# Routing by replaced maxima, filler products in TensorE's waits, a first gather in four PSUM banks, and the norm's factors moved

## The chip, the cores and the metric

The kernel runs on one core of a Trainium2 chip, in one launch. Its time is the device time of that core in microseconds (us). One core's TensorE (PE), VectorE (DVE), ScalarE (ACT) and GpSimd (POOL) work beside each other, each in the order of its own program; SyncE (SP) issues nearly all of the DMAs, in order, and DMAs are also issued from POOL.

## The reference

Two transformer blocks run one after the other over 256 tokens of width 1024, in fp32. The last part of the second block is a mixture of 32 experts, and the change lies where that part begins:

```python
h = layer_norm(DEEPNORM_ALPHA * h + m, ln1_g[l], ln1_b[l])
f = moe_ffn(h, ...)
h = layer_norm(DEEPNORM_ALPHA * h + f, ln2_g[l], ln2_b[l])

# moe_ffn
logits = (t @ w_router + b_router).astype(jnp.float32)     # 32 experts
top_val, top_idx = lax.top_k(logits, TOP_K)                # 4 of them for a token
gate_w = jax.nn.softmax(top_val, axis=-1)
hb = xb @ w_exp_in[e] + b_exp_in[e]                        # xb: the tokens of expert e
g = jnp.minimum(hb[:, :D_FF_2], SWIGLU_LIMIT)
u = jnp.clip(hb[:, D_FF_2:], -SWIGLU_LIMIT, SWIGLU_LIMIT)
a = g * jax.nn.sigmoid(SWIGLU_ALPHA * g) * (u + 1.0)
return a @ w_exp_out[e] + b_exp_out[e]
y = jnp.einsum('nk,nkd->nd', gate_w, y_slot)
```

Every expert has 12 MB of weights, and all 32 are read from HBM.

## The kernel before

**Weights.** `Stream` (`ws`) holds all weights as a list of 2 MB tiles: 42 of the dense stages, then six for each of the 32 experts (four for the hidden layer, two for the output). A tile goes to SBUF when one of the buffers in the list `ws.free` is named for it; SP issues the loads in that order, in `ahead` (L69). Each load waits until the buffer's former reader is done. Ten buffers hold expert tiles: three `ring` buffers `w0` to `w2`, three `wh0` to `wh2` that held split halves in the dense stages, `ring2` (`w`, which holds the gates `gt` until L832 has read them), `ring3` (`w`), and two in the pool `more4` (L1030), which is opened where the buffers of the earlier stages were closed. The first two experts are fixed, so their weights need no routing; for the others SP reads the expert's number from `ids` (L152).

**The stage before the experts** (t is a block of 128 tokens, 0 or 1). `rows_n` (L264) ends the product with `w_out` in four PSUM banks `acc`. L894 adds ALPHA times the block's input into `xn` on DVE and sums it. PE turns `xn` to feature-major (L900), ACT or DVE copies that to `zt` (L902, L904), ACT squares for the variance (L907), POOL takes the power -0.5 (L189), and PE multiplies `zt` with the router's weights (L912). The norm's factors are already in `wrg`; what they add to the logits is in `cr`, from eight products of L843. On DVE, L914 and L865 make the normed rows `hn` with both factors, whose rows `ln` POOL loads as 128 copies (L840).

**Routing.** `chosen(t)` ends the logits (L868, L869), takes the eight largest (L870), their places (L871), compares the places of the first four with 0 to 31 (L872) and adds them up to `sel` (L874). L923 and L925 count the tokens of each expert ahead of each token, L927 makes positions of that, and `one_hots` (L882) makes the selection matrix of experts 0 and 1. `gather(0)` (L1051) picks their tokens with 16 products, each out of 128 features and two token blocks. Then the four gate weights (L936 to L945, in buffers of the pool `rp`), `sort_experts` (L964 to L991, experts in order of their count), and the gates' rows (L1058) come before the first expert.

**The experts.** For each expert `hidden` multiplies the picked tokens with the weights (L1073), `gated` applies the activation (L1090 to L1100), `out_rows` (L1109) and `scatter` (L1124) end it. Experts have 32, 64 or 128 slots (`SLOTS`); experts of less than 128 slots use two or four parts of the array at once. `SORT` lists the places inside the experts' loop where a further step of `sort_experts` is put. Within each engine the order is set by a scheduler, apart from blocks under `manual_schedule` and waits put in by `after`.

## Time and profile before

| | |
|---|---|
| median of 3 runs | 1451.88 us (1450.11 to 1451.99) |
| profiled execution, its own time | 1451.97 us |
| its span from the first to the last instruction | 1450.2 us |
| TensorE busy | 1378.8 us (95%) |
| VectorE busy | 661.0 us (46%) |
| ScalarE busy | 429.4 us (30%) |
| GpSimd busy | 35.6 us (2%) |
| HBM read | 492.68 MB |
| mean over the span | 340 GB/s |

TensorE's busy time counts matmuls that are pipelined and whose ends are modelled, so a high share does not show that TensorE is the limit. The dense stages take about the first 500 us of the span, the experts nearly all of the rest.

### The profile page before, as it was taken

Reading aid. Unit: us, or ns where it says so; the run is one execution under the profiler, and the core shown is the slowest. Engines: PE = TensorE matmul, PEld = TensorE weight load, DVE = VectorE, ACT = ScalarE, POOL = GpSimd, SP = SyncE. Lnnn points to the kernel's source line nnn. Section 1 sums busy time; section 2 is a strip of 40 time slices with the busy share of each in tenths; the row PEclk is TensorE's granted clock in tenths of the full one; section 3 lists DMA queues with packets and bytes.
Section 4 is the critical chain, followed back from the end, with each engine's and each line's share of the span. In section 5 each row is a group of like instructions: output and inputs, shape, how many; then the busy total and the mean of one; then the engine's idle time right before and its main releaser. Section 6 shows DMA issues by size and latency. Waiting matters only on the chain. (4 is left out here: it accounts for less than half of the span.)

```text
span 1450.2 us, 21020 instructions
## 1 busy us (share of the span) xinstructions
PE 1378.8 (95%) x8401; PEld 869.7 (60%) x8402; DVE 661.0 (46%) x1614; ACT 429.4 (30%) x805; POOL 35.6 (2%) x53
## 2 busy tenths in 40 slices
PE   8999999999999989999999999999999999998884
PEld 7988999979999844444444444453544444443432
DVE  5868877865776543233233223233223333232223
ACT  4535655544664212121112112112111121211112
POOL 1001000010001000000000000000000000000000
PEclk9999999999999999999999999999999999999998
DMA  8434554445535989999999999999999999999995
GB/s 353 155 146 176 220 195 175 180 178 191 204 125 183 394 357 402 425 427 426 427 428 426 426 427 428 427 426 427 426 428 427 426 428 426 425 428 427 425 427 213
DMA packets 38007, 495.15 MB, mean 341 GB/s; under 512 B 4560, under 2 KB 4880, under 8 KB 8592
## 3 DMA queue, kind: packets, MB, share of 16 engines
q1 hardware_dynamic: 35424, 486.69, 81.1%
q0 software_dynamic: 2192, 6.88, 1.4%
q8 instruction: 68, 1.11, 0.3%
q14 instruction: 35, 0.29, 0.1%
q10 hardware_dynamic: 288, 0.18, 0.0%
HBM read 492.68 MB, written 1.05 MB: 340 GB/s over the span
## 5 line engine op out<-in xcount | busy, mean ns | idle before, releaser
L1073 PE MATMUL m<-w,xs 128*64 128x512 f32 (+2 forms) x1456 | 316.0, 601 | 12.6 <-DMA w<-in_wexp_dram 12.6
L1090 DVE TENSOR_TENSOR gu<-m,bexp 128x256 f32<-128x256 f32 (+2 forms) x128 | 51.2, 400 | 431.6 <-PE m L1087 282.9
L1073 PEld LDWEIGHTS m<-w,xs 128*64 128x64 f32 (+2 forms) x1456 | 101.9, 134 | 179.6 <-issue 169.9
L1076 ACT COPY hs<-m 128x512 f32<-128x512 f32 x128 | 75.1, 586 | 440.4 <-PE m L1073 440.4
L232 PE MATMUL b<-ah,wh 128*128 128x256 f32 x1552 | 195.4, 283 | 1.8 <-ACT wh L83 1.4
L232 PEld LDWEIGHTS b<-ah,wh 128*128 128x128 f32 x1552 | 188.3, 191 | 5.6 <-ACT wh L83 1.8
L105 DVE TENSOR_TENSOR wh<-w,wh 128x1024 fp32r<-128x1024 f32 (+1 forms) x152 | 174.3, 1180 | 28.2 <-ACT wh L104 28.2
L104 ACT ACTIVATE wh<-w 128x1024 fp32r<-128x1024 f32 (+1 forms) x154 | 148.9, 1020 | 87.9 <-PE b L232 53.4
L1109 PE MATMUL m<-w,ea 128*32 128x512 f32 (+2 forms) x704 | 154.0, 619 | 7.1 <-DMA w<-in_wexp_dram 4.4
L1073 PE MATMUL m<-wh,xs 128*32 128x512 f32 (+2 forms) x592 | 112.0, 597 | 2.3 <-DMA wh<-in_wexp_dram 2.3
L232 PE MATMUL b<-al,wh 128*128 128x256 f32 x776 | 100.6, 282 | 0.0
L1097 ACT ACTIVATE ea<-gu 128x128 f32<-128x128 f32 (+2 forms) x128 | 38.5, 301 | 209.4 <-DVE gu L1095 209.4
L205 DVE SCALAR_TENSOR_TENSOR one<-m,gs,one 128x512 fp32r<-128x512 f32 x64 | 46.8, 749 | 114.3 <-ACT one L204 112.8
L232 PEld LDWEIGHTS b<-al,wh 128*128 128x128 f32 x776 | 95.7, 192 | 0.0
L1109 PEld LDWEIGHTS m<-w,ea 128*32 128x32 f32 (+2 forms) x704 | 45.4, 133 | 83.5 <-issue 62.9
L1124 PE MATMUL acc<-one,so 128*128 128x512 f32 x256 | 78.3, 425 | 11.3 <-ACT one L204 10.1
L1085 PEld LDWEIGHTS m<-fold,hs 128*128 128x128 f32 x448 | 54.6, 192 | 46.9 <-issue 34.1
L1124 PEld LDWEIGHTS acc<-one,so 128*128 128x128 f32 x256 | 43.0, 188 | 51.6 <-ACT one L204 32.0
L1109 PE MATMUL m<-wh,ea 128*64 128x512 f32 (+2 forms) x320 | 70.4, 611 | 2.7 <-DMA wh<-in_wexp_dram 2.3
L204 ACT ACTIVATE one<-m,gs 128x512 fp32r<-128x512 f32 x64 | 42.5, 686 | 94.3 <-PE m L1109 94.3
L1073 PEld LDWEIGHTS m<-wh,xs 128*32 128x32 f32 (+2 forms) x592 | 33.7, 126 | 59.2 <-issue 57.2
L1051 PE MATMUL m<-oneh,hn 128*128 128x96 f32 (+2 forms) x480 | 64.5, 283 | 0.0
(358 smaller groups left out, 1351.0 us busy)
## 6 DMA issues: line engine op xcount, KB each, us to landing
w<-in_wexp_dram SPq DMA_DIRECT2D x134, 2048.0 KB, 27.2
wh<-in_wexp_dram SPq DMA_DIRECT2D x57, 2048.0 KB, 27.8
w<-in_wpre_dram SPq DMA_DIRECT2D x37, 2048.0 KB, 7.9
w<-in_wpre_dram SPq DMA_DIRECT2D x4, 512.0 KB, 7.8
w<-in_wexp_dram SPq DMA_DIRECT2D x4, 512.0 KB, 30.1
tab<-in_tab_dram SPq DMA_DIRECT2D x1, 1152.0 KB, 10.2
xn<-in_x_dram SPq DMA_DIRECT2D x2, 512.0 KB, 4.8
ra<-in_rowv_dram POOLq DMA_DIRECT2D x2, 512.0 KB, 7.1
```

Source lines behind the costliest of these rows:

```text
L104: self.nc.scalar.activation(h[:, c], t[:, c], AF.Copy)
L105: self.nc.vector.tensor_tensor(l[:, c], t[:, c], h[:, c].bitcast(F32), op=OP.subtract)
L204: return (A.activation(hi, src, AF.Copy, scale=scale), V.scalar_tensor_tensor(lo, src, scale, hi.bitcast(F32), op0=OP.mult, op1=OP.subtract))
L205: V.scalar_tensor_tensor(lo, src, scale, hi.bitcast(F32), op0=OP.mult, op1=OP.subtract))
L232: T.matmul(p[:, m, :], x[:, k, c], y[:, k, :], start=i == m == k == 0, stop=i == 2 and k == nk - 1, skip_group_check=True)
L1051: T.matmul(b[:, kk], hn[:, t, f], oh[:, t].rearrange("p i c -> p (i c)")[:, 128 - c0:128 + c1], start=t == 0, stop=t == 1)
L1073: T.matmul(b[g * c:(g + 1) * c], xs[:, k, :], w[:, kk, :], start=k < n, stop=k >= 8 - n, skip_group_check=True)
L1076: A.copy(h, b)
L1085: T.matmul(p[:, j, :], h[:, j * 128:(j + 1) * 128], fold, start=True, stop=True)
L1090: V.tensor_tensor(both, p[:, :, 0:c], bexp[:, r, f].rearrange("p j i -> p (j i)")[:, :, None].to_broadcast([128, 4, c]), op=OP.add)
L1109: T.matmul(ys[n][g * c:(g + 1) * c], ac[:, kk, :], w[:, kk, n * 512:(n + 1) * 512], start=(j == kk == 0) if c == 128 else j < 64 // c, sto ...
L1124: T.matmul(acc[t][n], so[:, t * 128:(t + 1) * 128], y[:, n, :], start=first and y is yh, stop=last and y is yl, skip_group_check=True)
```

## The change

- **Router.** The norm's two factors go to other places. `wsum` adds up `wrg` over the eight feature groups on DVE, so that `cr` needs one product and not eight. Mean and variance come from `bn_stats`, not from sums and ACT's squares. The eight router products write four parts of one bank, and a product with `fold` adds the four parts.
- **Rows.** `hn` is the normed row without factors, made by ACT. The 128 copies of the factors' rows are not loaded. The first four experts' tokens get the factors per feature when they are copied from PSUM (`factored`); `hn` itself gets them in a later step of `sort_experts`, from two single rows that PE spreads over the partitions.
- **Selection.** `chosen` replaces the four largest logits by a very small number (`match_replace`) and compares with the logits. The softmax works on all 32 logits, with the others multiplied by zero, in the experts' loop.
- **First gather.** Block 0 is counted, placed and picked ahead of block 1, into the four banks that held `acc`; block 1 adds to them.
- **Order.** `awake` multiplies `ones` with `iota` into banks that nobody reads then, at three places. Of `sort_experts` the counts and comparisons come early, `ids` inside the first expert's first hidden product, the rest in the loop. The pool `more4` is opened on the other side of SBUF.

```diff
-SORT = ((0, 1), (0, 2), (2, 1), (2, 3), (18, 1), (20, 1))
+SORT = ((0, 1), (0, 2), (0, 3), (2, 1), (2, 3), (18, 1), (20, 1))
...
-    ln = single.tile([128, 2, D], F32, name="one")
     ws.free.append((ring2, "w"))
-    for i in range(2):
-        nc.gpsimd.dma_start(ln[:, i, :], a["rowv"][4 + i:5 + i, :].to_broadcast([128, D]))
+
+    wsum = rp.tile([128, 2, E], F32, name="wsum")
+    V.tensor_reduce(wsum, wrg.rearrange("p i k e -> p i e k"), axis=AX.X, op=OP.add)
     cs = ps.tile([128, 2, E], F32, name="b")
-    for k in range(8):
-        T.matmul(cs, ones, wrg[:, :, k, :], start=k == 0, stop=k == 7)
+    T.matmul(cs, ones, wsum, start=True, stop=True)
...
         V.max(v8[:, t, :], logits[:, t, :])
-        V.max_index(i8[:, t, :], v8[:, t, :], logits[:, t, :])
-        V.tensor_tensor(oneh[:, t], iota[:, None, 0:E].to_broadcast([128, K4, E]),
-                        i8[:, t, 0:K4, None].to_broadcast([128, K4, E]), op=OP.is_equal)
-        return V.tensor_reduce(sel[:, t, :], oneh[:, t].rearrange("p k e -> p e k"), axis=AX.X, op=OP.add)
...
+        V.memset(v8[:, t, K4:], 3.4e38)
+        V.match_replace(left[:, t, :], v8[:, t, :], logits[:, t, :], -3.4e38)
+        return V.tensor_tensor(sel[:, t, :], logits[:, t, :], left[:, t, :], op=OP.is_gt)
...
+    def pick(t, ks):
+
+        for k in ks:
+            done = T.matmul(picked[k // 2][:, k % 2 * 128:k % 2 * 128 + 128], hn[:, t, k * 128:(k + 1) * 128],
+                            first[:, t].rearrange("p i c -> p (i c)")[:, 128 - caps(0):128 + caps(1)],
+                            start=t == 0 and k % 2 == 0, stop=t == 1, skip_group_check=True)
+        return done
+
+    def awake(b, n=1):
+
+        for _ in range(n):
+            done = T.matmul(b[:, 0:256], ones, iota[:, 0:256], start=True, stop=True, skip_group_check=True)
+        return done
...
+        for n in range(2):
+            V.scalar_tensor_tensor(xn[:, t, half[n]], xn[:, t, half[n]], ALPHA, acc[t][n], op0=OP.mult, op1=OP.add)
+            V.bn_stats(st[:, n, :], xn[:, t, half[n]])
+        V.bn_aggr(mean[:, t, :], st.rearrange("p n s -> p (n s)"))
...
-        with after(*[copied] if t else ()):
-            A.activation(junk, xn[:, t, :], AF.Square, bias=nmu[:, t:t + 1], accum_out=ve)
...
+                grouped = T.matmul(b[g:g + E], wrg[:, 0, k, :], zt[:, k, t * 128:(t + 1) * 128], start=k < 4, stop=k > 3, skip_group_check=True)
...
+            behind = grouped, T.matmul(b, groups, fold, start=True, stop=True)
...
-        V.scalar_tensor_tensor(hn[:, t, :], xn[:, t, :], nmu[:, t:t + 1], ln[:, 0, :], op0=OP.add, op1=OP.mult)
...
+        with after(copied if t else summed):
+            A.activation(hn[:, t, :], xn[:, t, :], AF.Identity, scale=lr[t], bias=minus[:, t:t + 1])
+        if t:
+            places_of(0, ahead[0])
+        chosen(t)
+    picked = acc[0] + acc[1]
+    with after(behind[1]):
+        done = pick(0, range(5))
     with after(done):
...
+        ahead = prefix(1)
+    placed = places_of(1, ahead[0])
+    with after(ahead[1]):
+        done = pick(0, range(5, 8))
     with after(done):
...
+        done = awake(ps.tile([128, 256], F32, name="b"))
+    with after(done):
+        pick(1, range(8))
...
+    more = pool(ctx, "more4", side="right")
...
+            if scalar:
+                A.activation(xs[:, k, :], src(k), AF.Identity, scale=g, bias=b)
+            else:
+                done = V.tensor_scalar(xs[:, k, :], src(k), g, b, op0=OP.mult, op1=OP.add)
...
+        for i, op in enumerate((OP.mult, OP.add)):
...
+                T.matmul(b, ones[32 * i:32 * i + 1, :], bw[32 * i:32 * i + 1, half[n]], start=True, stop=True)
+                for t in range(2):
+                    V.tensor_tensor(hn[:, t, half[n]], hn[:, t, half[n]], b, op=op)
```

The first place is SP's queue where the last of the expert loads of the dense stages and the two into `more4` stand. Before (`wh0` to `wh2` are the former halves, `w0_5361` and `w1_5363` are the two buffers of `more4`; a wait on DMAHW is on an earlier load of that semaphore):

```order
L69 DMA w1_5119<-in_wexp_dram 128x4096 [waits DMAHW6_49,DVE_49]
L69 DMA w_5359<-in_wexp_dram 128x4096 [waits DMASW3_49,DMASW4_49,DMASW2_49,DMASW5_49,DMASW1_49,DMASW6_49,DMASW0_49,DMASW7_49,PE_49,Pool_49]
L69 DMA wh0_5353<-in_wexp_dram 128x4096 [waits PE_49]
L69 DMA wh1_5355<-in_wexp_dram 128x4096 [waits PE_49]
L69 DMA wh2_5357<-in_wexp_dram 128x4096 [waits PE_49]
L69 DMA w0_5361<-in_wexp_dram 128x4096 [waits DMASW4_49,DMASW5_49,DVE_49,DMASW6_49,PE_49,DMAHW7_49,Activation_49,Pool_49]
L69 DMA w1_5363<-in_wexp_dram 128x4096 [waits DMAHW0_49]
L152 TENSOR_LOAD ids_4736 [waits DMASW3_49,DMASW2_49,DMASW4_49,DMASW1_49,DMASW5_49,DMASW0_49,DMASW6_49,DVE_49,DMASW7_49,Activation_49,Pool_49]
```

The same place of the changed kernel, where the load after the two into `more4` is `w2_5373`:

```order
L70 DMA w1_5111<-in_wexp_dram 128x4096 [waits DMAHW6_49,DVE_49]
L70 DMA wh0_5337<-in_wexp_dram 128x4096 [waits PE_49]
L70 DMA wh1_5339<-in_wexp_dram 128x4096 [waits PE_49]
L70 DMA wh2_5341<-in_wexp_dram 128x4096 [waits PE_49]
L70 DMA w0_5345<-in_wexp_dram 128x4096 [waits DMAHW7_49,PE_49,Activation_49]
L70 DMA w1_5347<-in_wexp_dram 128x4096 [waits DMAHW0_49]
L70 DMA w2_5373<-in_wexp_dram 128x4096 [waits DMAHW1_49,PE_49]
L153 TENSOR_LOAD ids_4736 [waits DMASW3_49,DMASW2_49,DMASW4_49,DMASW1_49,DMASW5_49,DMASW0_49,DMASW6_49,DVE_49,DMASW7_49,Activation_49,Pool_49]
```

The first load into `more4` no longer waits for DVE or POOL, only for PE and ACT, and one more load stands ahead of the reading of `ids`, where ten register loads stood ahead of that load before.

The second place is DVE from the end of the selection of block 1 to the last op that `rp` holds. Before (`hn_4720` rows are L865, `ex` and `oneh_5128` lie in `rp`):

```order
L874 TENSOR_REDUCE sel_4732<-oneh_5128 128x32 [waits DVE_49]
L865 SCALAR_TENSOR_TENSOR hn_4720<-hn_4720,l11_5227,one_5027 128x512
L927 SCALAR_TENSOR_TENSOR pg_4729<-b_5251,sel_4732 128x64 [waits DVE_49,PE_49]
L882 TENSOR_SCALAR oneh_5256<-iota_4721,pg_4729 128x128 [waits DVE_49]
L882 TENSOR_SCALAR oneh_5256<-iota_4721,pg_4729 128x128 x3
L865 SCALAR_TENSOR_TENSOR hn_4720<-hn_4720,l11_5227,one_5027 128x512
L932 COPY posm_4731<-pg_4729 128x2x2
L936 TENSOR_TENSOR ex_5263<-v8_5126 128x8
```

In the changed kernel, the same stretch (`left` is the row with its four largest replaced, `b_5266` the count ahead):

```order
L866 MAX v8_5116<-pg_4729 128x8 [waits DVE_49]
L867 MEMSET v8_5116 128x4 [waits DVE_49]
L868 MATCH_REPLACE left_5117<-v8_5116,pg_4729 128x32 [waits DVE_49]
L869 TENSOR_TENSOR sel_4732<-pg_4729,left_5117 128x32 [waits DVE_49]
L902 SCALAR_TENSOR_TENSOR pg_4729<-b_5266,sel_4732 128x32 [waits DVE_49,PE_49]
L878 TENSOR_SCALAR oneh_5118<-iota_4721,pg_4729 128x128 [waits DVE_49]
L878 TENSOR_SCALAR oneh_5118<-iota_4721,pg_4729 128x128
L991 TENSOR_SCALAR ea_5299<-b_5269,sortc_4727 32x32 [waits DMASW1_49,DMASW6_49,PE_49,Activation_49]
L993 SCALAR_TENSOR_TENSOR ea_5299<-b_5269,sortc_4727 32x32
L994 TENSOR_TENSOR ea_5299<-ea_5299 32x128 [waits DVE_49]
L1007 TENSOR_SCALAR xs0_5303<-acc01_5035,colv_68 128x128 [waits PE_49]
```

No op on `hn` and no gate weight stands there any more, and two of the four one-hot ops are gone from behind block 1's count.

The third place is PE from the gather to the first hidden product. Before (`acc00`, `acc01` serve as the gather's banks; the counts L923, L925 and L964 stand ahead):

```order
L1051 MATMUL acc00_5284<-oneh_5256,hn_4720 128x128 [waits DVE_49]
L1051 MATMUL acc01_5285<-oneh_5256,hn_4720 128x128
L1051 MATMUL acc01_5285<-oneh_5256,hn_4720 128x128 [waits DVE_49]
L1051 MATMUL acc01_5285<-oneh_5256,hn_4720 128x128 x6
L1051 MATMUL acc00_5284<-oneh_5256,hn_4720 128x128 [waits DVE_49]
L1051 MATMUL acc00_5284<-oneh_5256,hn_4720 128x128 x6
L978 MATMUL m_5317<-ones_69,ea_5303 128x2 [waits DVE_49,Activation_49]
L986 MATMUL m_5333<-perm_5321,ea_5303 32x32 [waits DVE_49]
L987 MATMUL m_5333<-perm_5321,cn_5299 32x32
L1058 MATMUL m_5340<-gtok_4730,oneh_5256 128x2 x2
L1058 MATMUL m_5346<-gtok_4730,oneh_5256 128x2 x2
L1073 MATMUL m_5352<-w2_4908,xs0_5307 64x512 [waits DMAHW7_49,PE_49,Activation_49]
```

In the changed kernel (block 1's counts, and ahead of them five of block 0's eight picks, stand just ahead; L916 is a filler of `awake`, L1145 the first hidden product):

```order
L908 MATMUL acc10_5036<-oneh_5118,hn_4720 128x128
L908 MATMUL acc11_5037<-oneh_5118,hn_4720 128x128 x2
L916 MATMUL b_5280<-iota_4721,ones_69 128x256
L908 MATMUL acc00_5034<-oneh_5118,hn_4720 128x128 [waits DVE_49,Activation_49]
L908 MATMUL acc00_5034<-oneh_5118,hn_4720 128x128
L908 MATMUL acc01_5035<-oneh_5118,hn_4720 128x128 x2
L908 MATMUL acc10_5036<-oneh_5118,hn_4720 128x128 x2
L908 MATMUL acc11_5037<-oneh_5118,hn_4720 128x128 x2
L1025 MATMUL m_5329<-ones_69,ea_5299 128x2 [waits DVE_49,DMASW5_49,PE_49,Pool_49]
L1145 MATMUL m_5336<-w2_4908,xs0_5303 64x512 [waits DMAHW7_49,Activation_49]
```

Behind block 1's count stand 11 picks and a filler instead of 16 picks, and the sort's two products and the gates' four have moved behind the first hidden products.

## Rows read from the trace of the kernel before

**Rows 1.** The page: what the DMA engines moved, GB/s in 40 slices of the span

```profile
GB/s 353 155 146 176 220 195 175 180 178 191 204 125 183 394 357 402 425 427 426 427 428 426 426 427 428 427 426 427 426 428 427 426 428 426 425 428 427 425 427 213
```

**Rows 2.** Stretches: us, busy us and count by engine, granted clock, DMA share, GB/s

```profile
464.00:478.60 14.60, 14.60 (x121) 14.34 (x120) 14.60 (x36) 7.58 (x12) 0.00 (x0) 1.00 0.76 290
...
483.00:500.00 17.00, 17.00 (x79) 13.87 (x78) 1.67 (x6) 2.32 (x4) 1.62 (x3) 1.00 1.01 424
...
511.00:518.00 7.00, 6.04 (x42) 5.76 (x42) 4.91 (x21) 0.79 (x2) 0.00 (x0) 0.74 0.45 142
518.00:560.00 42.00, 41.23 (x215) 18.87 (x215) 14.42 (x55) 6.45 (x13) 0.00 (x0) 1.00 0.99 408
...
600.00:1000.00 400.00, 393.57 (x2000) 186.96 (x1998) 118.35 (x396) 69.43 (x142) 0.00 (x0) 1.00 1.01 427
1000.00:1400.00 400.00, 378.09 (x2076) 170.35 (x2072) 121.08 (x416) 71.33 (x148) 0.00 (x0) 0.99 1.01 427
```

**Rows 3.** What SP's queue waited for, 460 to 560 us: total, times, longest

```profile
SPq L69 <- DVE pg L944: 13.9, 1, 13.9
...
SPq L69 <- DVE one L832: 6.6, 1, 6.6
...
SPq L152 <- DVE ids L988: 2.5, 1, 2.5
```

**Rows 4.** SP's timeline, single loads: start, duration of the issue

```profile
477.69 0.33 SPq L69 DMA_DIRECT2D w<-in_wexp_dram  x1
...
500.63 0.33 SPq L69 DMA_DIRECT2D wh<-in_wexp_dram  x1
...
515.15 0.33 SPq L69 DMA_DIRECT2D w<-in_wexp_dram  x1
...
524.82 0.33 SPq L69 DMA_DIRECT2D w<-in_wexp_dram  x1
...
551.30 0.33 SPq L69 DMA_DIRECT2D wh<-in_wexp_dram  x1
```

**Rows 5.** DMA issues: count, KB each, median us to landing

```profile
one<-in_rowv_dram POOLq DMA_DIRECT2D x2, 512.0 KB, 13.1
```

**Rows 6.** DVE's groups by shape, 463 to 520 and 1400 to 1451 us: busy, mean ns

```profile
L874 DVE TENSOR_REDUCE sel<-oneh 128x32 f32<-128x128 f32 x2 | 0.7, 368 | 0.1
...
L944 DVE TENSOR_REDUCE pg<-oneh 128x64 f32<-128x256 f32 x1 | 0.6, 590 | 0.0
...
L871 DVE FIND_INDEX8 i<-v,logits 128x8 uint32<-128x32 f32 x2 | 0.4, 179 | 0.0
...
L1183 DVE BATCH_NORM_STATS2 st<-acc 128x6 f32<-128x512 f32 x2 | 1.3, 690 | 0.9 <-PE acc L1124 0.9
```

**Rows 7.** Timeline of the routing, 475 to 527 us: start, duration

```profile
475.43 1.89 PE L843 MATMUL b<-wrg,ones 128*128 128x64 f32 x16
...
502.22 0.68 DVE L894 SCALAR_TENSOR_TENSOR xn<-xn,acc 128x512 f32<-128x512 f32 x1
...
504.61 1.15 ACT L907 ACTIVATE al<-xn,nmu 128x1024 f32<-128x1024 f32 x1 [1.22 <-DVE nmu L896]
...
507.73 0.57 POOL L189 TENSOR_TENSOR l<-ve,mhalf 128x1 f32<-128x1 f32 x1
...
509.47 0.37 DVE L874 TENSOR_REDUCE sel<-oneh 128x32 f32<-128x128 f32 x1
...
511.83 5.16 PE L1051 MATMUL acc<-oneh,hn 128*128 128x128 f32 x32
...
519.38 7.09 PE L1073 MATMUL m<-w,xs 128*64 128x512 f32 x32
```

**Rows 8.** Short stretches of the routing, columns as in rows 2

```profile
506.00:507.00 1.00, 0.41 (x4) 0.30 (x3) 1.00 (x7) 0.00 (x0) 0.00 (x0) 1.00 1.12 475
...
508.00:510.00 2.00, 0.11 (x1) 0.11 (x1) 1.54 (x7) 0.00 (x0) 0.29 (x1) 0.50 1.03 434
...
515.00:517.00 2.00, 2.00 (x19) 1.88 (x18) 0.15 (x1) 0.59 (x1) 0.00 (x0) 1.00 0.56 106
```

More of the change, by code (lines that the diff above doesn't have):

```diff
@@ L910, in build @@
+        if t:
+            with after(grouped):
+                ahead = prefix(0)
+            with after(ahead[1]):
+                kept = awake(acc[1][0])
+        groups = rp.tile([128, 128], F32, name="groups")
+        summed = (V.tensor_copy if t else A.copy)(groups, b)
         b = ps.tile([128, E], F32, name="b")
-        for k in range(8):
-            T.matmul(b, zt[:, k, t * 128:(t + 1) * 128], wrg[:, 0, k, :], start=k == 0, stop=k == 7)
+        with after(*[kept] if t else ()):
+            behind = grouped, T.matmul(b, groups, fold, start=True, stop=True)
@@ L1125, in scatter @@
                              stop=last and y is yl, skip_group_check=True)
[L1127 to L1128 removed]
     pend = None
+    done = []
     sort = sort_experts()
[L1131 to L1133 removed]
+    todo = iter(())
+    next(sort)
     for r in range(E):
```

237 lines of the change are left out of this document (129 added, 108 removed).

## The prediction

> **What bounds the kernel now.** The page's line of rates comes first [rows 1]: from the 17th slice to the last but one the DMA engines move 425 to 428 GB/s, with hardly a break. The stretches say it more exactly [rows 2]: 427 GB/s over 600 to 1400 us, with the DMA share at 1.01. The experts' time is the time of reading their weights; a tile of 2 MB (2.097 MB) takes 2.097 / 0.427 = 4.91 us. TensorE reads as nearly always busy too, but it is behind the loads at first and catches up later, so it counts only where it gives a buffer back late. The end therefore moves by what the DMA queue loses or saves, and by nothing else.
>
> Call the experts' loads e1, e2, ... in SP's order. Eight are issued in the dense stages, the last at 500.63; the next, e9 and e10, go into `more4`, and e9 is issued at 515.15 [rows 4]. SP's longest wait of that stretch is 13.9 us for L944, the gate weights' last reduce [rows 3]: `more4` lies over buffers that the routing still reads. The queue was full to 511, then 511 to 518 ran at 142 GB/s [rows 2]: 7.0 x (1 - 142/427) = 4.67 us are lost. That is the one hole. The stretch 518 to 560 runs at 408 GB/s, with a full share: 42 x (1 - 408/427) = 1.87 us more, with few loads waiting in the queue.
>
> The routing behind it: the last half of `xn` is added at 502.22, block 1's selection ends at 509.84, the gather runs from 511.83 and the first hidden product at 519.38 [rows 7]. The granted clock fell to 0.50 in 508 to 510, after PE was busy 0.41 us of 506 to 507, and was 1.00 again in 515 to 517 [rows 8]; 0.50 is 1.2 GHz, 1.00 is 2.4.
>
> **The change part by part.**
>
> *The rows of the factors.* Two transfers of 512 KB [rows 5] go. They were issued from POOL at about 483, where the queue was full at 424 GB/s [rows 2], so each byte pushed a weight back: 2 x 0.524 MB / 0.427 = 2.46 us. The two single rows that come instead are 8 KB, under 0.1 us. In their place a rule of the Trainium skill could be put (DMA: Bandwidth & Descriptors, Specifications), which gives HBM a limit of about 358 GB/s for a core. By it these transfers would be worth 2.9 us, and the sum below would be 0.5 us lower. The rows show 427 GB/s for 800 us, so the measured rate decides.
>
> *`wsum`.* A reduce of 512 elements on DVE is not in the trace. Between 128 and 256 elements the price rises from 0.37 to 0.59 us [rows 6], so 512 cost about 1.03; it is at least 0.59, and I bound it above by 1.5. It stands ahead of L832 (now L836), and e3 waits for L832 until 477.69 [rows 3, 4]. In 464 to 478.6 DVE is busy for all of the 14.6 us, and the DMA share is 0.76, in 483 to 500 it is 1.01 [rows 2]: the reduce delays e3, and with it the whole stream, by its 1.03 us. On PE one product replaces eight: 1.89 us [rows 7] become about 0.24, which gives PE 1.65 us.
>
> *The release of `more4`.* The loads now wait for PE and ACT alone, that is for the last readers of `xn` and `zt`: the grouped router products and the ACT op that makes `hn` of block 1. In that chain ACT's square is gone. PE's 1.65 us go into a wait of PE for block 0's copies, since block 0's router products now stand ahead of the last row products; so the last half of `xn` comes near 501.9, and not at 502.9. DVE then does bn_stats (0.69 [rows 6]), bn_aggr, the copy of a quarter of `zt` and block 0's selection between them: POOL's power ends near 505.0, where before it began at 507.73 [rows 7]. ACT's op on 1024 columns is 1.15 us [rows 7]: with DVE's small op ahead, done at 506.6. SP can issue e9 then, 8.5 us earlier.
>
> The queue ran dry at 511; now at 511 + 1.03 - 2.46 = 509.6. Some 1 us passes from issue to first bytes (515.15, and 106 GB/s in 515 to 517 [rows 8]), so e9 has to be issued by 508.6. It has 2.0 us to spare and the hole of 4.67 us closes. What it costs if that cover is gone: each us of e9 behind 508.6 is a us of the end.
>
> *The next waits.* With e9 and e10 the queue is filled to 509.6 + 9.8 = 519.4; e11 waits for the first two hidden products. So the start of expert 0 matters next. Block 1's selection: MATCH_REPLACE is not in the trace. Its nearest row is FIND_INDEX8, 0.18 us [rows 6]; I bound it from 0.18 to 0.6 (the 256-element reduce) and take 0.3. It replaces an index op, a compare and a reduce, 0.9 us together. With the products in four groups and no wait for POOL, selection ends near 507.1. Counting is 0.6 us of PE and 0.2 of DVE, the one-hots now two and not four: 508.5. PE then does three remaining picks, a filler and eight picks. Before, 32 rows took 5.16 us [rows 7], partly at the low clock, so 16 rows cost at most 2.6; at full clock I take 1.7, and 1.1 for the picks and filler ahead, in part beside the one-hots. The last pair's eviction is hidden behind the first hidden product's other features. Expert 0 starts near 511.0, 8.4 us ahead of 519.38. e11 can go at 514.9, needed by 518.4.
>
> The sort's products and the gates' move into expert 0 and cost PE about 1.5 us there. The register loads of `ids` on SP now come after e11: by the program's order 30 of them lie between e11 and e15. Ten stood between the wait of 2.5 us for `ids` and e11 before [rows 3, 4], at most (524.82 - 515.15 - 2.5) / 10 = 0.72 us each. So e15 can go by 514.9 + 21.6 = 536.5 at worst; it is needed near 538.
>
> e16, issued at 551.30 [rows 4], waits for the end of expert 0. It was needed at 516.1 + 7 x 2.097/0.408 = 552.1 less 1: it was just in time. Now it comes at 551.3 - 8.4 + 1.5 = 544.4 and is needed near 544. So PE allows about 6.9 + 0.5 = 7.4 us of gain and no more, and of the 1.87 us of the shallow queue I count 0.4 (bounds 0 and 1.87).
>
> *The rest is hidden.* The factors on `hn` (four one-row products, eight adds of about 0.7 us on DVE) come in expert 2. PE is idle for 6 of the 400 us from 600 on and 22 of the next 400 [rows 2], so it makes up for them there. If this cover were gone it would be about 3 us of PE and 5.6 of DVE, on a queue several loads deep. The eight evictions with factors instead of two cost each less than a quarter more. `bin` is loaded a little later and moves the same bytes.
>
> **The sum**, on the profiled execution's own 1451.97 (span 1450.2; the median shown is 0.09 below): -2.46 (rows) - 4.67 (hole) - 0.4 (shallow queue) + 1.03 (`wsum`) = -6.5. Predicted: **1445.5 us**. Bounds of the terms alone: `wsum` 0.59 to 1.5, queue 0 to 1.87, expert 0's end ±1.5: 1443.6 to 1447.
>
> **The rivals.** A difference under 0.2% (2.9 us) counts as none.
>
> *Expert 0 starts late (0.15).* If the fillers do not hold the clock at 2.4 GHz, picks, counts and the first hidden product run at 1.2, as the gather did in 508 to 514 [rows 8]. PE's 4.6 us of work from the first pick on double at most, and e16 gets 7.4 - 4.6 = 2.8 us: 1449.2 at worst, 1448 if it falls for a part. For it: PE has short waits for DVE throughout. Against it: rows products, router products and three fillers stand in these waits, and before it fell only after PE had been all but idle.
>
> *The release comes later (0.08).* If PE's wait of e9 counts to the last pick (510.8) instead of the router products, the hole keeps 2.2 us: 1447.7.
>
> *The change doesn't close the hole (0.07).* Another reader, say the DVE op on `rp`, holds `more4`, or the queue runs dry at e11 for as long as at e9. Then only the rows count, less `wsum`: -1.4, 1450.5.
>
> *Slower (0.05).* MATCH_REPLACE on DVE, twice in series, could be far dearer than the ops that it replaces. At 4.5 us each expert 0 starts where it does now, and the 1.5 us moved into it make e16 late. At 6.5 us each it starts 4 us later: e16 at 556.8, 5.5 later, and the queue with it, so about 1456. FIND_INDEX8 at 0.18 us on the same 32 columns speaks against it.
>
> **Chances.** The forecast has 0.65. Faster by over 0.2% are it, 0.09 of the late start and the later release: 0.65 + 0.09 + 0.08 = 0.82. Within 0.2%: the worst 0.06 of the late start and the open hole, 0.13. Slower 0.05. The range reaches from 1443.0 (the shallow queue gained in full) to 1448.8, which leaves out the open hole, the slower case and the worst of the late start.
>
> **What would show it.** Right: no stretch of 511 to 518 under 400 GB/s; e9 issued near 506.6 and not waiting for DVE; the first hidden product near 511; the granted clock 1.00 throughout; e3 near 478.7; above 420 GB/s from 483 on. Wrong: a clock of 0.50 in the routing, a hole ahead of e11 or e16, or a long MATCH_REPLACE.

## The result, and the profile after

The changed kernel took 1442.37 us (median of 4 runs, 1442.23 to 1442.79) against 1451.49 us (4 runs, 1450.11 to 1451.99): a ratio of 0.9934, 95% interval 0.992 to 0.9949. That is 9.1 us faster. The forecast was 1445.5 us in a range from 1443.0 to 1448.8: the direction was right, and the time lies 0.6 us below the range. The profiled execution took 1442.36 us with a span of 1440.6 us.

The stretches of the changed kernel, in the columns of [rows 2], and its line of rates, which answers to [rows 1]:

```profile
GB/s 358 167 139 180 224 185 176 182 178 193 197 133 167 385 426 398 426 428 427 427 425 426 427 427 426 427 427 426 424 425 428 424 427 427 426 427 425 428 427 225
```

```profile
464.00:478.60 14.60, 14.60 (x107) 13.73 (x107) 14.60 (x36) 6.13 (x10) 0.00 (x0) 1.00 0.84 303
483.00:500.00 17.00, 16.35 (x95) 12.78 (x93) 6.24 (x14) 3.06 (x5) 0.56 (x1) 1.00 1.00 430
...
511.00:518.00 7.00, 7.00 (x41) 2.85 (x37) 2.30 (x14) 1.43 (x3) 0.00 (x0) 1.00 1.01 422
518.00:560.00 42.00, 41.40 (x218) 19.44 (x219) 17.05 (x67) 7.70 (x17) 1.52 (x4) 1.00 1.00 417
```

The reader is to look at 511 to 518 first: 422 GB/s where 142 stood. The hole is closed. The granted clock is 1.00 there, where it was 0.74. The stretch 518 to 560 rose from 408 to 417, not to 427.

SP's waits from 460 to 560 us (total, times, longest), and its issues of e3, e9, e11, e15 and e16 (start and duration), which answer to [rows 3] and [rows 4]:

```profile
SPq L70 <- PE m L1038: 9.1, 1, 9.1
SPq L70 <- PE m L1183: 8.0, 1, 8.0
SPq L70 <- DVE one L836: 7.7, 1, 7.7
...
SPq L70 <- PE b L947: 2.5, 1, 2.5
SPq L70 <- ACT hn L964: 1.9, 1, 1.9
```

```profile
476.99 0.33 SPq L70 DMA_DIRECT2D w<-in_wexp_dram  x1
503.40 0.33 SPq L70 DMA_DIRECT2D w<-in_wexp_dram  x1
513.14 0.33 SPq L70 DMA_DIRECT2D w<-in_wexp_dram  x1
533.93 0.34 SPq L70 DMA_DIRECT2D wh<-in_wexp_dram  x1
542.53 0.33 SPq L70 DMA_DIRECT2D wh<-in_wexp_dram  x1
```

SP waits for PE's router products (L947) and ACT's `hn` (L964), no longer for VectorE's last reduce of the gates. SP's longest wait, 9.1 us, is that of e11, which is issued as the first hidden products end; the profile puts it down to L1038, a product of the sort beside them. e9 goes out at 503.40 and not at 515.15. The wait for L836 has grown from 6.6 to 7.7 us: that is `wsum`. The one to remember is L1183, expert 0's out products, for which e16 waits 8.0 us.

The timeline of the routing, which answers to [rows 7] (start, duration):

```profile
471.68 1.12 DVE L844 TENSOR_REDUCE wsum<-wrg 128x64 f32<-128x512 f32 x1
...
502.13 1.24 ACT L964 ACTIVATE hn<-xn,minus,l 128x1024 f32<-128x1024 f32 x1 [1.67 <-DVE minus L962]
...
503.37 0.09 DVE L868 MATCH_VALUE_LOAD left<-v,pg 128x8 f32 x1
503.45 0.18 DVE L868 MATCH_REPLACE8 left<-v,pg 128x32 f32<-128x32 f32 x1
503.66 0.19 DVE L869 TENSOR_TENSOR sel<-pg,left 128x32 f32<-128x32 f32 x1
...
509.44 3.65 PE L1145 MATMUL m<-w,xs 128*64 128x512 f32 x16
```

Block 1's selection ends at 503.85, and the first hidden product starts at 509.44 instead of 519.38. e3, expert 0's start, e11 and e16 are 1.6 to 1.9 us earlier than forecast, the selection and e9 3.2. The larger part of that stands ahead of the change: e1 was issued at 463.44 in this execution and at 465.15 in the profiled one of before.

So the times were split at marks that don't hang on the start. The DMA records of a trace give each load's landing (the end of its last packet). The table gives e1's issue, then the stages: from e1's issue to e3's, from there to e14's landing, to e16's landing, to that of e190 (almost the last whole load), the sum of these four ("stream"), then from e190's landing to the first store of the output ("tail"), what is left, and the execution's own time. The first two rows are means over four profiles of before and five of the changed kernel (the repeats are told below), with the extremes of the stream.

```
                 e1    e1-e3  e3-e14 e14-e16 e16-e190  stream  tail  rest  own time
before (4)      464.25  12.54  70.63  10.55   858.76   952.47  22.32 11.77  1450.82   stream 952.05 to 952.96
after (5)       463.61  13.56  62.00  10.84   859.53   945.93  21.78 11.62  1442.93   stream 945.69 to 946.11
difference       -0.64  +1.02  -8.63  +0.29    +0.77    -6.54  -0.54 -0.15    -7.89
rows_back       462.49  13.56  64.81   9.93   859.61   947.91  23.62 11.62  1445.63
release_late3   464.08  13.56  66.38   9.94   859.54   949.42  21.73 11.56  1446.79
cs_eight        463.53  12.53  62.20  13.28   859.50   947.51  22.89 11.72  1445.65
wsum_late       465.36  12.53  62.11  11.81   859.89   946.34  22.74 11.67  1446.11
last_first      464.93  13.56  62.05   9.81   859.74   945.15  21.91 11.66  1443.65
combined        464.77  12.53  61.98   9.83   859.78   944.12  22.00 11.73  1442.62
two_moves       463.34  12.53  62.18   9.81   859.77   944.29  23.44 11.64  1442.71
no_fillers      464.24  13.56  62.06  11.29   859.85   946.77  21.52 11.54  1444.07
warm_start      464.99  13.56  61.94  10.90   859.72   946.12  21.25 11.76  1444.12
start9_after    463.79  13.56  62.03  10.82   859.86   946.27  21.28 11.61  1442.95
start9_before   465.84  12.53  70.08  11.06   858.84   952.51  21.89 11.73  1451.96
```

In all profiles of either kernel the stream stays within 0.5 us of its mean. It is 6.54 us shorter after the change; the forecast said 6.5 for the end. What the forecast lacks lies ahead of e1 and behind e190.

### The profile page after: what moved, and what is told of

It reads as the page before. It is cut to its first block, busy times and chain, and to the rows that moved or that the text cites. A ratio compares the mean times of both kernels' runs of the same rounds, so it can differ in the third digit from the quotient of the medians.

```text
span 1440.6 us, 21051 instructions
## 1 busy us (share of the span) xinstructions
PE 1377.1 (96%) x8407; PEld 864.3 (60%) x8408; DVE 664.9 (46%) x1627; ACT 431.3 (30%) x810; POOL 35.7 (2%) x53
## 3 DMA queue, kind: packets, MB, share of 16 engines
HBM read 491.64 MB, written 1.05 MB: 342 GB/s over the span
## 5 line engine op out<-in xcount | busy, mean ns | idle before, releaser
L1145 PE MATMUL m<-w,xs 128*64 128x512 f32 (+2 forms) x1456 | 315.7, 600 | 7.2 <-DMA w<-in_wexp_dram 7.2
L1145 PEld LDWEIGHTS m<-w,xs 128*64 128x64 f32 (+2 forms) x1456 | 101.2, 133 | 173.4 <-issue 166.4
L1183 PE MATMUL m<-w,ea 128*32 128x512 f32 (+2 forms) x704 | 156.4, 631 | 6.4 <-DMA w<-in_wexp_dram 3.7
L1145 PE MATMUL m<-wh,xs 128*32 128x512 f32 (+2 forms) x592 | 110.8, 597 | 2.3 <-DMA wh<-in_wexp_dram 2.3
L1183 PEld LDWEIGHTS m<-w,ea 128*32 128x32 f32 (+2 forms) x704 | 46.3, 135 | 83.9 <-issue 67.9
L1183 PE MATMUL m<-wh,ea 128*64 128x512 f32 (+2 forms) x320 | 74.1, 657 | 4.1 <-DMA wh<-in_wexp_dram 2.3
L1145 PEld LDWEIGHTS m<-wh,xs 128*32 128x32 f32 (+2 forms) x592 | 33.6, 126 | 58.8 <-issue 57.5
```

The source lines that it names most:

```text
L1145: T.matmul(b[g * c:(g + 1) * c], xs[:, k, :], w[:, kk, :], start=k < n, stop=k >= 8 - n, skip_group_check=True)
L1183: T.matmul(ys[n][g * c:(g + 1) * c], ac[:, kk, :], w[:, kk, n * 512:(n + 1) * 512], start=(j == kk == 0) if c == 128 else j < 64 // c, sto ...
```

## The experiments

Medians below stand beside runs of before on the same chip. A single execution scatters by 2 us and more either way, so most readings rest on the stages of the table. No changed kernel was timed on the chip of wsum_late, last_first, combined and warm_start.

**Repeats of both kernels.** No edit. after_again, after_third and after_fifth were timed; before_again, before_third, before_fourth and after_fourth are single profiles.

> The changed kernel as it is, beside five more runs of the kernel before. In the two profiles the loads' lead of the changed kernel is already 1.7 us ahead of the first expert's load, in stages that the change does not touch: there the profiled run of before has TensorE's first products 0.212 us apart until 16 us, that of after 0.113 us apart from 10 us on. Theory A (this is luck of an execution): times of before scatter over some 1.9 us, with about 1450 where the products are fast early, and the changed kernel scatters as much, 1442.2 to 1444.1; against equal starts the change is worth 7.4 to 7.8 us. Theory B (the whole 9.1 us come from the change): both kernels repeat within 0.6 us of their medians, the gap stays 9 us, and the start of this profile is at full speed in after each time.

> The kernel before as it is, one more profile. From the issue of e1 to the landing of the last whole load the profiles of before and of the changed kernel differ by 6.7 to 6.8 us; the other 2 us and more lie ahead of e1 and behind that landing. Theory A (those are an execution's luck): e1 to last landing is 952.5 again within 0.5, and e1's issue (465.15 in the first profile) falls among those of the changed kernel's variants, 462.5 to 465.4. Theory B (the change shortens what lies outside as well): e1 is again later than in the changed kernel on the same chip by 1 us and more, or the tail (last whole landing to first output, 22.5) longer than its 21.3 to 23.6.

> The kernel before, a third profile, beside three more of before and of the changed kernel on one chip. From e1 to the last whole landing all profiles of before give 952.5 to 953.0 and of the changed kernel 945.7 to 946.3; that part is 6.7. Theory A (the rest of the 9 us is an execution's luck in TensorE's clock): e1's issue is spread alike for both kernels, 463.3 to 465.9, and the tail (last whole landing to first output) alike, 21.3 to 23.6. Theory B (part of it comes from the change): both of before's e1, or both of its tails, lie above both of the changed kernel's by 0.5 us and more.

> The same kernel and the same two theories as for before_third: e1's issue in 463.3 to 465.9 and the tail in 21.3 to 23.6 for either kernel (A), or above the changed kernel's by 0.5 us and more (B).

> The changed kernel, on the chip of before_third, timed against more runs of before. Theory A: over enough runs the gap of the medians falls from 9 towards 6.7, and the fastest runs of both differ by 6.7 within 0.5. Theory B: the gap of the medians stays at 8 to 9.

> The same kernel and the same two theories as for after_third, one profile: e1's issue and the tail spread as those of before (A) or below both of them by 0.5 us and more (B).

> The changed kernel on the same chip as two_moves, for the comparison: stream from e1's issue to the last whole landing 945.9 within 0.3, median 1442.4 to 1444.1. Against before: if the rest of the gap is luck alone, a gap of 6.7 to 8; if it is systematic, 8.5 to 9.3 again.

Measured: after_again 1442.6 us against 1451.42 (11 runs of before, 1449.02 to 1453.49), ratio 0.9941 [0.9927, 0.9954]; after_third 1444.07 against 1453.08 (8 runs), 0.9941 [0.9925, 0.9958]; after_fifth 1443.71 against 1453.16 (11 runs), 0.9941 [0.9927, 0.9955]. The single profiles took 1449.88, 1451.88 and 1449.53 us for before and 1443.77 for after_fourth.

The start of the four profiles of before shows two cases. PE's first projections, in the first profile of before and in before_again (start, duration):

```profile
10.27 2.04 PE L232 MATMUL b<-ah,wh 128*128 128x256 f32 x8 [1.42 <-ACT wh L83]
```

```profile
10.26 1.15 PE L232 MATMUL b<-ah,wh 128*128 128x256 f32 x8 [1.42 <-ACT wh L83]
11.25 1.07 PE L232 MATMUL b<-al,wh 128*128 128x256 f32 x8
```

The same eight products take 2.04 or 1.15 us: full speed came at 16.4 us in the first and by 10.3 in the second, after the same instructions. The records of the granted clock agree: they begin with 1.00 at 16.3 us in the first trace and at 9.2 in the second (ahead of its first record the profile prints 1.00 as well). e1 was issued at 465.15 and 463.35. before_third is like the first (465.27), before_fourth is early (463.24). For the changed kernel e1 lies at 463.06 to 464.21, but wsum_late, whose program is the same up to there, has 465.36 with full speed from 16.3 us. Up to 440 us every engine runs the same instructions in the same order in the profiles of before and of the changed kernel, and one program gives an early and a late e1. The start is therefore an execution's luck, as theory A says.

That TensorE's clock alone decides it is not shown. Of the sixteen profiles without products put ahead of the start, the three with full speed from 16.3 us on have e1 at 465.15 to 465.36, the other thirteen (from 8.4 to 14.7 us on) at 462.49 to 464.93. But among the thirteen the two do not go together: before_fourth is slow until 14.5 us and has its e1 at 463.24.

The tail is a second case of it. PE's last products for the hidden features, in the changed kernel and in rows_back:

```profile
1412.82 1.92 PE L1145 MATMUL m<-w,xs 128*32 128x512 f32 x16 [0.34 <-DMA w<-in_wexp_dram]
1414.67 1.97 PE L1159 MATMUL m<-fold,hs 128*128 128x32 f32 x16
```

```profile
1414.63 2.67 PE L1148 MATMUL m<-w,xs 128*32 128x512 f32 x16 [1.99 <-DMA w<-in_wexp_dram]
1417.23 3.62 PE L1162 MATMUL m<-fold,hs 128*128 128x32 f32 x16
```

The 16 products with `fold` took 1.97 or 3.62 us. The stretches of rows_back around them, and those of the changed kernel at the same distance from e190's landing:

```profile
1410.40:1415.40 5.00, 3.01 (x28) 1.47 (x24) 1.04 (x5) 0.84 (x2) 0.00 (x0) 1.00 1.00 415
1415.40:1420.40 5.00, 5.00 (x27) 3.33 (x20) 0.93 (x5) 0.84 (x2) 0.00 (x0) 0.53 0.86 350
1420.40:1425.40 5.00, 5.00 (x27) 1.51 (x30) 1.14 (x6) 0.26 (x1) 0.00 (x0) 0.50 0.57 228
```

```profile
1409.26:1414.26 5.00, 4.66 (x36) 1.94 (x27) 1.03 (x5) 0.84 (x2) 0.00 (x0) 0.74 1.01 418
1414.26:1419.26 5.00, 3.91 (x36) 2.38 (x32) 2.07 (x10) 1.10 (x3) 0.00 (x0) 0.94 0.88 357
1419.26:1424.26 5.00, 4.49 (x24) 1.12 (x16) 0.00 (x0) 0.48 (x1) 0.00 (x0) 0.72 0.54 218
```

The granted clock of rows_back falls to 0.53 and 0.50 (1.2 GHz) for ten us in which PE has the most to do, after a stretch in which it worked 3.01 of 5 us. In the changed kernel it fell one load earlier, while PE would have waited for a load anyway, and was back at 0.94. The tails are 23.6 and 21.5 us long. The clock records of all twenty profiles bear this out. In twelve the clock falls to 0.50 from 2.0 to 0.2 us ahead of e190's landing, and the tail lasts 21.3 to 22.1 us. In the other eight it falls 3.7 to 5.4 us behind it, and the tail lasts 21.5 to 23.6: 22.7 to 23.6 in the four in which it then stays at 0.50 for ten us. Two of the four profiles of before belong to the eight, and one of the five of the changed kernel.

Theory B is not refuted, though. The medians differ by 9.1, 8.8, 9.0 and 9.45 us in four comparisons: theory A expected the gap to fall towards 6.7, or to 8 at most, and it stayed near 9, as theory B said. The profiles' mean differs by 7.9, the fastest run of each kernel (1448.89 and 1442.12) by 6.8. All but the stream's 6.5 is where luck was seen. The gap lies in the scatter: 62 timed runs of before reach from 1448.89 to 1456.57 (the middle half 1450.4 to 1453.5), 19 of the changed kernel from 1442.12 to 1445.65 (1442.5 to 1444.1). All four profiles of before, 1449.53 to 1451.97, lie below the median of these runs, 1452.0. So no trace shows where a run above it loses its time, and why the kernel before scatters more stays open.

**The factors' rows.** rows_back is the changed kernel with

```diff
+    ln = single.tile([128, 2, D], F32, name="one")
     ws.free.append((ring2, "w"))
+    for i in range(2):
+        nc.gpsimd.dma_start(ln[:, i, :], a["rowv"][4 + i:5 + i, :].to_broadcast([128, D]))
```

> The changed kernel with the two 512 KB broadcasts loaded again at their old place, into a buffer that nothing reads. Sum of the prediction: +2.46 us, since each byte pushes a weight back: 1444.8, and the landings from e4 to e8 later by 2.5. Rival 1 (the bytes cost more than their share, 2.7 us by the two profiles, as a broadcast that is moved slowly): +2.7 to 3.5, 1445.1 to 1445.9. Rival 2 (the queue has slack there): within 0.5 of 1442.4.

Measured: 1446.04 us (6 runs, before 1451.42), ratio 0.9967 [0.9955, 0.9979]. From e3's issue to e14's landing it is 2.81 us longer than the changed kernel. The three loads e4 to e6 land 5.79, 6.46 and 5.26 us behind one another and not 4.86 each: 2.93 us. In before they took 5.92, 6.28 and 5.26. Rival 1 is right: the rows cost 2.9, not 2.46. The stream is only 1.98 us longer, as the stage behind e14 is 0.91 shorter. The edit moved a second thing there: the scheduler set expert 0's last products behind fewer hidden products of expert 1, and e16 goes out 1.7 us earlier counted from e1. That lies behind e4 to e6, so the 2.9 us stand. The median rose by 3.4 beside after_again, more than the stream; the profiled execution has an early e1 and a tail of 23.62.

**The hole.** release_late3 puts e9's release later:

```diff
-    close(xp)
-    more = pool(ctx, "more4", side="right")
...
+    with after(scaled[0]):
+        for _ in range(3):
+            A.activation(xn[:, 0, :], xn[:, 1, :], AF.Copy)
+    close(xp)
+    more = pool(ctx, "more4", side="right")
...
```

(the pool stands behind the evictions of the first gather there; `scaled[0]` is the last of these on ACT).

> The changed kernel with more4 given back late: three ScalarE copies of 1024 columns that read xn stand behind the evictions of the first gather, so that e9 is issued near 511.7 instead of 503.4, and nothing else moves. Sum of the prediction: e8 lands at 508.7, an isolated load lands 7.4 us behind its issue, 519.1 against 514.3, so the hole is open again by 4.7 us: 1447.1. Rival 1 (the closed hole is not what gave the time): 1442.4 to 1443. Rival 2 (part of it is given back later, by the thin queue that follows): +3.0 to 4.0, 1445.4 to 1446.4.

e9's issue and the two stretches around it:

```profile
512.26 0.33 SPq L70 DMA_DIRECT2D w<-in_wexp_dram  x1
```

```profile
508.00:510.00 2.00, 0.89 (x9) 0.73 (x7) 1.49 (x6) 1.97 (x4) 0.00 (x0) 1.00 0.68 281
...
511.00:518.00 7.00, 7.00 (x38) 2.46 (x35) 1.84 (x11) 2.42 (x5) 0.00 (x0) 1.00 0.69 246
```

Measured: 1446.71 us (6 runs), ratio 0.9967 [0.9955, 0.9979]. The hole is back at the same place; e3 to e14 is 4.38 us longer, and the stage behind it 0.90 shorter, as e16 is no longer late for the stream. The stream is 3.5 us longer, the median 4.1 beside after_again: Rival 2, with the sum's mechanism.

**`wsum` and the eight products.** cs_eight undoes the reduce; wsum_late moves it.

```diff
-    wsum = rp.tile([128, 2, E], F32, name="wsum")
-    V.tensor_reduce(wsum, wrg.rearrange("p i k e -> p i e k"), axis=AX.X, op=OP.add)
...
-    T.matmul(cs, ones, wsum, start=True, stop=True)
+    for k in range(8):
+        T.matmul(cs, ones, wrg[:, :, k, :], start=k == 0, stop=k == 7)
```

> The changed kernel with the reduce on VectorE undone: eight products on TensorE as before, no wsum. Sum of the prediction: e3 is issued 1.03 us earlier and the stream with it, -1.0: 1441.4; TensorE's 1.65 us more are hidden as e9 is issued with 3 us and more to spare. Rival 1 (the reduce was hidden; e3's delay of 1.0 in the two profiles is something else): 1442.4. Rival 2 (TensorE's 1.65 us reach the end by expert 0's end and e16): 1443 to 1444.

```diff
-    V.tensor_reduce(wsum, wrg.rearrange("p i k e -> p i e k"), axis=AX.X, op=OP.add)
+    with after(mixed):
+        V.tensor_reduce(wsum, wrg.rearrange("p i k e -> p i e k"), axis=AX.X, op=OP.add)
...
-    T.matmul(cs, ones, wsum, start=True, stop=True)
+    with after(rowed):
+        T.matmul(cs, ones, wsum, start=True, stop=True)
```

(`mixed` is the mixing's last op on VectorE, `rowed` the last of the first row products, which stand ahead of `wsum` in the program there.)

> The changed kernel with the reduce wsum moved on VectorE behind the last op of the mixing, and its product behind the first row products; TensorE's work is otherwise the same. e3 is issued 1.0 us earlier for certain. Theory A (as cs_eight suggests, the end hangs on e16, which waits for TensorE's last products of expert 0 and lands 7.4 us behind its issue): TensorE is no earlier, e16 lands where it does, 1442.1 to 1442.9, no gain. Theory B (the sum of the prediction: the stream moves with e3): -1.0, 1441.6.

Measured: cs_eight 1445.5 us (5 runs, before 1451.42), ratio 0.9956 [0.9942, 0.9969]; wsum_late 1443.91 us (6 runs, before 1452.59), 0.994 [0.9925, 0.9955]. Both issue e3 1.03 us earlier, as the table's second column shows, and in both the gain is gone at e16. Its issue in cs_eight, and in after_again on the same chip:

```profile
544.14 0.33 SPq L70 DMA_DIRECT2D wh<-in_wexp_dram  x1
```

```profile
543.00 0.33 SPq L70 DMA_DIRECT2D wh<-in_wexp_dram  x1
```

Each lands 7.40 us behind that, an isolated load. In cs_eight TensorE carries the eight products and gives e16's buffer back later: e14 to e16 takes 13.28 us and not 10.84, the stream is 1.6 longer than the changed kernel's. Rival 2's mechanism is right, and the -1.0 of the sum wrong; the median rose by 2.9 beside after_again, above Rival 2's 1443 to 1444, and this profile's tail is 1.1 longer than the changed kernel's. In wsum_late TensorE is no earlier, and the stream does not gain (946.34): theory A, though the median lies 1.0 above the times that it gave.

**e16's buffer.** last_first moves one thing on PE: expert 0's last eight products ahead of most of expert 1's hidden products, which wait for them (`out` is the last product of `out_rows`).

```diff
-                T.matmul(b[g * c:(g + 1) * c], xs[:, k, :], w[:, kk, :], ...)
+                with after(*behind if k > 1 else ()):
+                    T.matmul(b[g * c:(g + 1) * c], xs[:, k, :], w[:, kk, :], ...)
...
-        h = hidden(xs, c, iter(()) if r else sort)
+        h = hidden(xs, c, iter(()) if r else sort, (out,) if r == 1 else ())
...
-            h2 = hidden(xs, c)
+            h2 = hidden(xs, c, behind=(out,) if (r, f) == (1, 1) else ())
```

> The changed kernel with one thing moved: the last eight products of expert 0 (which free the buffer that e16 takes) stand behind 8 hidden products of expert 1, not behind 25. Theory A (e16's issue sets the stream): e16 issued near 538.5 instead of 542.5 to 543.0, e15 lands 4.9 us behind e14 (5.7 in the changed kernel) and e16 4.9 to 5.0 behind e15 (5.1 to 5.3), -1.1: 1441.5. Theory B (thin queue from another cause): e15 still takes 5.7 us, 1442.6.

PE at that place in the changed kernel, and in last_first:

```profile
535.02 0.59 PE L1183 MATMUL m<-wh,ea 128*64 128x512 f32 x1
535.03 3.59 PE L1145 MATMUL m<-wh,xs 128*64 128x512 f32 x14
538.03 0.59 PE L1145 MATMUL m<-w,xs 128*64 128x512 f32 x1
538.45 0.59 PE L1145 MATMUL m<-wh,xs 128*64 128x512 f32 x1
538.46 2.31 PE L1145 MATMUL m<-w,xs 128*64 128x512 f32 x9
540.60 1.89 PE L1183 MATMUL m<-wh,ea 128*64 128x512 f32 x8
```

```profile
537.80 0.59 PE L1184 MATMUL m<-wh,ea 128*64 128x512 f32 x1
538.23 0.59 PE L1146 MATMUL m<-w,xs 128*64 128x512 f32 x1
538.23 1.87 PE L1184 MATMUL m<-wh,ea 128*64 128x512 f32 x6
539.52 0.59 PE L1146 MATMUL m<-wh,xs 128*64 128x512 f32 x1
539.94 0.59 PE L1184 MATMUL m<-wh,ea 128*64 128x512 f32 x1
```

Measured: 1443.21 us (6 runs, before 1452.59), ratio 0.9933 [0.9919, 0.9947]. Its marks lie 1.5 us later than the changed kernel's first profile from e1 on, so e16, at 540.57, is 3.5 us earlier. e15 lands 4.91 us behind e14 (5.67 in the changed kernel) and e16 4.90 behind e15 (5.17): e14 to e16 is 1.03 us shorter, and the stream 0.78. Theory A holds for the loads; its 1441.5 us did not come.

**Both moves.** combined has wsum_late, last_first and 16 products at the start (as in warm_start); two_moves has the first two.

> The changed kernel with the three edits together: products of ones at the start, wsum later, the last products of expert 0 earlier. Theory A: with e16 no longer late the 1.0 us of wsum reaches the end: -1.1 -1.0, and up to -0.5 from the start: 1440.0 to 1440.6. Theory B (the stages are independent of e16): wsum alone counts, 1441.5.

> The changed kernel with wsum later and the last products of expert 0 earlier, without products at the start. By the stream of combined (944.1 from e1's issue to the last whole landing, against 945.9 as the mean of four profiles of the changed kernel): e1 to e3 12.53, e14 to e16 9.8, stream 944.1, and a median 1.8 us below after_fifth. Rival (the scatter of the start and the tail covers it, or the edits take back what they give behind e16): stream 945 and more, median within 0.5 of after_fifth.

Measured: combined 1442.45 us (6 runs, before 1452.59), ratio 0.9929 [0.9915, 0.9943]; two_moves 1443.06 us (6 runs, before 1453.16), 0.9935 [0.9921, 0.9949]. One run of two_moves took 2328.57 us; the median of its other five is 1442.91. The 1440.0 to 1440.6 forecast for combined did not come. The streams are 944.12 and 944.29 us, 1.8 and 1.6 below the changed kernel, so with e16 early most of the 1.0 us of e3 does get through. Beside after_fifth (1443.71) two_moves gains 0.65 us at the end, less than the runs can tell; its profile has a tail of 23.44 us. It is the better stream, not a shown better time.

**TensorE's start.** 16 (warm_start) or 9 (start9) unread products stand ahead of the first transposes:

```diff
+WARM = 16
...
+    for _ in range(WARM):
+        T.matmul(xp4[0][:, 0, 0:128], ones, ones, start=True, stop=True, skip_group_check=True)
```

> The changed kernel with 16 unread 128 x 128 products of ones ahead of the first transposes, in the 4 us in which TensorE waits for the first load. Theory A (the executions differ by when TensorE reaches full speed: 10.2 us in one profile of the changed kernel, 14.7 in another, 16.4 in that of before): full speed by 10 us at the latest in each run, e1 issued near 463.2, 1441.8 to 1442.3, and the runs scatter less than the 2.1 us of the changed kernel. Theory B (the scatter comes from elsewhere, as from the loads): 1442.6, with the same scatter.

> The kernel before with 9 unread products of ones ahead of the first transposes (16 took 6.4 us, too long; 9 end as the first load lands). Full speed from the first projection on, thus e1 near 463.4. Theory A (luck of the start makes part of the gap): 1450.2, about 1.3 us below before, with a smaller scatter. Theory B: as before.

> The changed kernel with the same 9 products. Theory A: with the start equal on both sides the gap to start9_before is the 6.7 us of the stream between e1 and the last landing, within 1. Theory B (more than the stream's terms came from the change): the gap is 8 to 9 us.

Measured: warm_start 1444.19 us (before 1452.59), ratio 0.9944 [0.993, 0.9958]; start9_before 1453.95 us (12 runs, before 1451.34), 1.0015 [1.0003, 1.0027]; start9_after 1445.02 us (5 runs), 0.9949 [0.9932, 0.9967]. PE in warm_start, and in start9_before:

```profile
1.10 6.35 PE L339 MATMUL b<-ones 128*128 128x128 f32 x32 [1.10 <-DVE mhalf L168]
7.28 1.91 PE L342 MATMUL b<-ident,xn 128*128 128x128 f32 x16
```

```profile
10.38 1.98 PE L233 MATMUL b<-ah,wh 128*128 128x256 f32 x8 [2.29 <-ACT wh L84]
12.16 1.87 PE L233 MATMUL b<-al,wh 128*128 128x256 f32 x8
```

The 16 ran 6.35 us, too long, and put the transposes off by 2.2. With 9, start9_before's transposes were faster, and then PE waited 2.29 us for ACT and its projections came at half speed until 13.9. start9_after held full speed from 5.2 us on, and its e1 is at 463.79, no earlier than without the products. The products don't take the luck away, so the test of an equal start did not come about. The gap of the two medians is 8.9 us, as theory B said, that of the streams 6.2. My expectations for these three failed.

**The fillers.** no_fillers leaves out the three unread products of `awake`.

> The changed kernel without its three unread products of iota in TensorE's waits. The prediction: they hold the clock; its rival of a late expert 0 gave up to 4.6 us of doubled TensorE work. Theory A (without them the granted clock falls to 0.50 in the routing, expert 0's products run at half speed for some us): e16 issued 2 to 4.6 us later, 1444.5 to 1447. Theory B (rows, router and picks alone hold the clock): the clock stays 1.00, expert 0 starts 1 us earlier, 1442.0 to 1442.6.

The stretches 505 to 508 and 508 to 510 of no_fillers, and of the changed kernel:

```profile
505.00:508.00 3.00, 3.00 (x21) 2.87 (x20) 1.21 (x6) 0.00 (x0) 0.59 (x1) 0.50 0.98 412
508.00:510.00 2.00, 2.00 (x12) 2.00 (x11) 0.00 (x0) 0.36 (x2) 0.00 (x0) 0.50 1.03 434
```

```profile
505.00:508.00 3.00, 3.00 (x24) 2.81 (x24) 1.60 (x7) 1.17 (x4) 0.52 (x1) 1.00 1.01 423
508.00:510.00 2.00, 0.89 (x7) 0.57 (x8) 1.32 (x6) 0.45 (x2) 0.00 (x0) 1.00 0.97 406
```

Measured: 1443.24 us (5 runs, before 1451.34), ratio 0.9937 [0.992, 0.9955]. Without them the clock falls to 0.50, and expert 0 starts at 512.63, 2.4 us later when e1's issue is taken off. That part of theory A is right. e16 is only 0.65 us later, since the scheduler set expert 0's last products behind fewer others there, as in rows_back; the stream loses 0.84 us, which the median does not show.

## Why the prediction was off

**The sum of the stream was right, in part by luck.** Its terms, beside what the profiles of the two kernels (means as above) give for them:

```
term                       forecast   measured   read from
wsum                        +1.03      +1.02     e1 to e3
rows of the factors         -2.46      -2.88     e4 to e6 land in 17.46, then 14.58 us
hole of more4               -4.67      -4.48     e8 and e9 land in 15.17, then 10.69 us
shallow queue               -0.4       -0.96     e11 to e16 land in 31.48, then 30.52 us
the rest                     0         +0.77     e16 to e190
sum                         -6.5       -6.53
```

That the sums agree to 0.03 us is luck: the rows and the shallow queue were worth 0.4 and 0.6 more than forecast, and 0.77 that was put at nothing takes them back. The measured terms are parts of the time line and not what each part of the change is worth alone: opening the hole again costs the stream 3.5 us, since the stage up to e16 gives 0.9 back.

*wsum.* Right: the reduce took 1.12 us on DVE, and e3 was 1.02 later. What the forecast did not see is that undoing it doesn't pay: PE's 1.65 us come back at e16.

*Rows.* Mis-sized by 0.4: "each byte pushed a weight back" at 427 GB/s is too cheap. 1.05 MB in 2.9 us is 362 GB/s. That comes near the figure by the Trainium skill (DMA: Bandwidth & Descriptors, Specifications) that the forecast set aside, some 358 GB/s for a core. The trace does not bear that limit out, as the weights still move at 427 GB/s; the rows are moved by POOL's queue in pieces of 4 KB beside packets of 16 KB, and what makes them dearer wasn't tried.

*Hole.* Right, mechanism and size; release_late3 opens it again. SP waits for PE's router products and ACT's `hn`, as said. e9 left 10.1 us earlier (from e1's issue: 50.06, then 39.97 us), not 8.5; it had 1.6 us more to spare than forecast.

*Shallow queue.* 0.96 and not 0.4. The limit by e16 was right: it goes out 7.3 us earlier counted from e1 (forecast 6.9), and is late for the stream by 1.0 us still, as last_first shows. The prediction's "just in time" for e16 before the change was misread: there too it lands 7.3 to 7.4 us behind its issue, as an isolated load, and e15 and e16 land 5.24 and 5.30 us behind the load ahead. The term itself was too small because the forecast took e11 to e14 as still slowed, and they now come at 4.90 to 4.95 us.

*Expert 0, selection, clock.* Expert 0 starts 8.2 us earlier counted from e1 (forecast 8.4); MATCH_REPLACE with its load took 0.27 us (0.3); the clock stayed at 1.00 in the routing, and no_fillers shows that the unread products hold it. These rivals are out.

*The rest.* Not free: 0.77 us. 0.2 are at e19 and e20 (`bout` and the two rows), 0.6 are spread over the later loads, a tenth of a us here and there. Which instruction causes them is not known.

**The step that failed** is the first: "The end therefore moves by what the DMA queue loses or saves, and by nothing else." The sum was set against one profiled execution as if its start and its tail were constants. They are not: e1 goes out between 463.2 and 465.3 us in four profiles of before, and the tail takes 21.8 to 22.8 there, up to 23.6 in variants, by when TensorE's clock falls. The profiled execution of before had a late start, that of the changed kernel an early one and a short tail: 1.7 + 1.0 us that no term held. Over repeats 1.3 us of this remain in the profiles (0.64 + 0.54 + 0.15) and 2.3 to 2.9 in the medians. So 1445.5 should have had this scatter in its range; the bounds of its terms alone ended at 1443.6. Whether part of the scatter's difference is due to the change is open.

## What to carry to other kernels

Split two profiles at the landing of named loads, and compare stage by stage: here the stream of each kernel stayed within 0.5 us of its mean while whole times scattered by 3 to 8 us. When a hole in a stream closes, look for the load that is next to wait for a buffer, and for what stands ahead of that buffer's last reader on its engine; here a gain of 1 us ahead of it was worth nothing in the stream until eight products were moved. Repeat the profile of the base before building a sum to a tenth of a per cent on it.
